# A 16-element average pool: loads and stores issued by GpSimd instead of SyncE, each as a single packet per DMA engine

## The chip, the cores and the metric

The kernel runs on one core of a Trainium2 chip. The metric is the device time of one execution in microseconds (us), and the time of a kernel is the median over several executions. One further execution is recorded by the hardware profiler, and every duration below comes from that record unless it is said otherwise.

Five engines work beside each other on a core, each through its own queue of instructions in program order: TensorE (PE), VectorE (DVE), ScalarE (ACT), GpSimd (POOL) and SyncE (SP). An instruction that has to wait for a semaphore holds up everything behind it in the queue of its engine. Copies between device memory (HBM) and on-chip memory (SBUF) are issued by an instruction on one of these queues and carried out by the 16 DMA engines of the core.

## The reference

The input `x` is float32 of shape 32 x 256 x 4096, and `output_size` is 256. Every output is the mean of 16 neighbouring inputs:

```python
for i in range(output_size):
    start = int(i * length / output_size)
    end = int((i + 1) * length / output_size)
    result[:, :, i] = np.mean(x[:, :, start:end], axis=-1)
```

So 134.2 MB are read and 8.4 MB are written, and each number that is read takes part in one addition.

## The kernel before

Batch and channel are one axis of 8192 rows. A tile holds 4 rows in each of the 128 partitions, which are 128 x 16384 numbers, 64 KB in each partition and 8.39 MB altogether. There are 16 tiles. Tiles 0 to 14 are one region of `x` (`x_many`), in which each partition owns 60 consecutive rows and tile `t` is the t-th group of 4 of them. Tile 15 is a region of its own (`x_last`). The pool of input buffers has `bufs=2`, so two tiles are on the chip at a time, and the load of tile t+2 has to wait until tile t has been read for the last time.

A tile is worked on in five steps:

- Line 70 loads it, one DMA of 128 rows of 64 KB.
- Line 73, on GpSimd, folds the second half of the tile's windows: it adds the upper 8 of the 16 numbers of each window onto the lower 8.
- Line 78, on VectorE, sums the first half's windows over all 16 numbers. It needs the load alone, and runs beside line 73.
- Line 81, on VectorE, sums the second half's windows over the 8 numbers that line 73 left. It is the last reader of the tile.
- Line 84, on ScalarE, multiplies the 1024 sums of each partition by 1/16 in place.

The sums of tiles 0 to 14 stay in `res_many` (60 KB in each partition) and those of tile 15 in `res_last` (4 KB in each partition). There are three stores, all through the helper at line 58. The first writes `res_many` in one DMA and stands in the code between the load of tile 15 and its arithmetic. The other two write partitions 0 to 119 and 120 to 127 of `res_last` at the end. Together they move 8.39 MB, as much as one tile. Each store raises the semaphore `stored`, for which SyncE waits at line 95 before the kernel ends.

The Tile layer decides the order of the instructions on each engine from the code, the buffers and its own estimates, and sets the waits. In the kernel before, SyncE holds only DMAs. The load of tile t+2 waits there for line 81 of tile t and for the landing of the load of tile t. VectorE's order is line 78 and line 81 of tile 0, then of tile 1, and so on. GpSimd holds only the 16 additions of line 73.

Of the kernel before, what the change touches and what calls it, by code (L numbers as in the profile page):

```python
# [1 line left out]

# [4 lines left out]


@with_exitstack
def kernel(  # L10
    ctx: ExitStack,
    tc: tile.TileContext,
    x: bass.AP,
    output_size: int,
    out: bass.AP,
):

    nc = tc.nc
    F32 = mybir.dt.float32
    X = mybir.AxisListType.X

    batch, channels, length = x.shape
    ob, oc, olen = out.shape
    assert ob == batch and oc == channels and olen == output_size
    assert length % output_size == 0
    window = length // output_size  # L30
    hw = window // 2
    inv_w = 1.0 / float(window)

    P = nc.NUM_PARTITIONS
    R = 4
    rows = batch * channels
    assert rows % (P * R) == 0
    ntiles = rows // (P * R)
    many = (ntiles - 1) * R
    cells = R * output_size  # L40
    m = cells // 2
    cols = R * length

    xr = x.rearrange("b c l -> (b c) l")
    orow = out.rearrange("b c o -> (b c) o")
    x_many = xr[0 : P * many, :].rearrange("(p r) l -> p (r l)", p=P, r=many)
    o_many = orow[0 : P * many, :].rearrange("(p r) o -> p (r o)", p=P, r=many)
    x_last = xr[P * many :, :].rearrange("(p r) l -> p (r l)", p=P, r=R)
    o_last = orow[P * many :, :].rearrange("(p r) o -> p (r o)", p=P, r=R)

    res_many = nc.alloc_sbuf_tensor("res_many", [P, (ntiles - 1) * cells], F32, align_bytes=256)
    res_last = nc.alloc_sbuf_tensor("res_last", [P, cells], F32, align_bytes=256)
    inpool = ctx.enter_context(tc.tile_pool(name="inpool", bufs=2))

    stored = nc.alloc_semaphore("stored")

    def store(out, in_):
        ins = nc.sync.dma_start(out=out, in_=in_)
        tc.no_tile_sem_insts.add(ins.ins.name)
        ins.then_inc(stored, 16)  # L60

    for t in range(ntiles):
        last = t == ntiles - 1
        xin = inpool.tile([P, cells, window], F32, name="xin")
        if last:
            res, base, src = res_last, 0, x_last
        else:
            res, base = res_many, t * cells
            src = x_many[:, t * cols : (t + 1) * cols]
        nc.sync.dma_start(out=xin.rearrange("p o w -> p (o w)"), in_=src)  # L70
        if last:
            store(o_many, res_many[:, :])
        nc.gpsimd.tensor_add(  # L73
            out=xin[:, m:cells, 0:hw],
            in0=xin[:, m:cells, 0:hw],
            in1=xin[:, m:cells, hw:window],
        )
        nc.vector.reduce_sum(  # L78
            out=res[:, base : base + m], in_=xin[:, 0:m, :], axis=X
        )  # L80
        nc.vector.reduce_sum(  # L81
            out=res[:, base + m : base + cells], in_=xin[:, m:cells, 0:hw], axis=X
        )
        nc.scalar.mul(  # L84
            out=res[:, base : base + cells],
            in_=res[:, base : base + cells],
            mul=inv_w,
        )
    for lo, hi in ((0, 120), (120, P)):
        store(o_last[lo:hi, :], res_last[lo:hi, :])  # L90

    ctx.pop_all().close()
    tc.close()
    tc.compile()  # L94
    nc.sync.wait_ge(stored, 48)
    nc.sync.sem_clear(stored)


# [1 line left out]
_INS = ['x', 'output_size']  # L100
_OUTS = [((32, 256, 256), 'float32')]

_NUMBERS = {'output_size': 256}


# [26 lines left out]
```

## Time and profile before

| | |
|---|---|
| median of 3 executions | 333.5 us (333.32 to 333.67) |
| the profiled execution | 333.37 us, of which the span of its record is 332.1 us |
| VectorE busy | 209.7 us (63% of the span) |
| GpSimd busy | 139.7 us (42%) |
| ScalarE busy | 18.2 us (5%) |
| DMA packets' time, share of 16 engines' span | 99.4% |
| moved | 142.61 MB, 429 GB/s over the span |

The span is the time from the first to the last recorded event on the core, and 1.27 us of the profiled execution's own time lie outside it. The median of the three executions is 0.13 us above the profiled one. Busy time is the time in which an engine computes; instructions that only issue a DMA, wait or branch are not counted in it. In the profile "SPq" and "POOLq" are the queues of SyncE and GpSimd, that is, their issuing and waiting instructions. `xin<-in_x_dram` is a load of line 70, `out_dram<-res_many` and `out_dram<-res_last` are stores of line 58.

### The profile page before, as it was taken

Reading aid. Unit: us, or ns where it says so; the run is one execution under the profiler, and the core shown is the slowest. Engines: PE = TensorE matmul, PEld = TensorE weight load, DVE = VectorE, ACT = ScalarE, POOL = GpSimd, SP = SyncE. Lnnn points to the kernel's source line nnn. Section 1 sums busy time; section 2 is a strip of 40 time slices with the busy share of each in tenths; the row PEclk is TensorE's granted clock in tenths of the full one; section 3 lists DMA queues with packets and bytes.
Section 4 is the critical chain, followed back from the end, with each engine's and each line's share of the span. In section 5 each row is a group of like instructions: output and inputs, shape, how many; then the busy total and the mean of one; then the engine's idle time right before and its main releaser. Section 6 shows DMA issues by size and latency. Waiting matters only on the chain.

```text
span 332.1 us, 160 instructions
## 1 busy us (share of the span) xinstructions
DVE 209.7 (63%) x32; ACT 18.2 (5%) x17; POOL 139.7 (42%) x20
## 2 busy tenths in 40 slices
DVE  0029396692939669293966939295693929569392
ACT  1000101001010100101010010101000010100001
POOL 0027091542709164270916427090643709063270
DMA  9898999989899998989899998989999898989997
GB/s 379 379 505 379 474 411 426 458 379 505 379 489 395 450 434 379 505 379 505 379 474 411 395 489 379 505 379 489 395 450 434 379 505 379 505 379 474 395 466 307
DMA packets 2599, 142.61 MB, mean 429 GB/s; under 512 B 295, under 2 KB 295, under 8 KB 423
## 3 DMA queue, kind: packets, MB, share of 16 engines
q1 hardware_dynamic: 2599, 142.61, 99.4%
HBM read 134.22 MB, written 8.39 MB: 429 GB/s over the span
## 4 chain that ended last, share of the span: by engine, by line
DMA 66%; POOL 18%; DVE 11%; POOLq 3%; issue 0%; ACT 0%; SPq 0%
DMA xin<-in_x_dram 66%; POOL xin L73 18%; DVE res_many L81 9%; POOLq L94 3%; DVE res_last L81 1%; ACT res_last L84 0%; SPq L70 0%; POOLq L73 0%
## 5 line engine op out<-in xcount | busy, mean ns | idle before, releaser
L73 POOL TENSOR_TENSOR xin<-xin 128x4096 f32<-128x4096 f32 x16 | 139.5, 8719 | 181.7 <-DMA xin<-in_x_dram 181.7
L78 DVE TENSOR_REDUCE res_many<-xin 128x512 f32<-128x8192 f32 x15 | 130.3, 8686 | 107.4 <-DMA xin<-in_x_dram 107.4
L81 DVE TENSOR_REDUCE res_many<-xin 128x512 f32<-128x4096 f32 x15 | 66.3, 4420 | 2.5 <-POOL xin L73 2.3
L84 ACT ACTIVATE res_many<-res_many 128x1024 f32<-128x1024 f32 x15 | 15.9, 1057 | 289.8 <-DVE res_many L81 289.8
L78 DVE TENSOR_REDUCE res_last<-xin 128x512 f32<-128x8192 f32 x1 | 8.7, 8686 | 6.3 <-DMA xin<-in_x_dram 6.3
L81 DVE TENSOR_REDUCE res_last<-xin 128x512 f32<-128x4096 f32 x1 | 4.4, 4420 | 0.2 <-POOL xin L73 0.2
L84 ACT ACTIVATE res_last<-res_last 128x1024 f32<-128x1024 f32 x1 | 1.1, 1057 | 18.5 <-DVE res_last L81 18.5
L84 ACT ACT_TABLE_LOAD x1 | 1.3, 1283 | 0.7 <-PEq L113 0.7
L113 POOL MEMSET const-float32-0.0<- 128x1 f32 x1 | 0.1, 99 | 0.2 <-issue 0.2
L113 POOL MEMSET const-bfloat16-1.0<- 128x1 bf16 x1 | 0.1, 103 | 0.0
L113 POOL MEMSET const-uint8-127<- 128x1 uint8 x1 | 0.1, 103 | 0.0
L113 POOL MEMSET const-float32-1.0<- 128x1 f32 x1 | 0.1, 99 | 0.0
## 6 DMA issues: line engine op xcount, KB each, us to landing
out_dram<-res_many SPq DMA_DIRECT2D x1, 7680.0 KB
out_dram<-res_last SPq DMA_DIRECT2D x1, 480.0 KB
xin<-in_x_dram SPq DMA_DIRECT2D x16, 25.3
out_dram<-res_last SPq DMA_DIRECT2D x1, 32.0 KB
```

Source lines behind the costliest of these rows:

```text
L73: nc.gpsimd.tensor_add(out=xin[:, m:cells, 0:hw], in0=xin[:, m:cells, 0:hw], in1=xin[:, m:cells, hw:window],)
L78: nc.vector.reduce_sum(out=res[:, base : base + m], in_=xin[:, 0:m, :], axis=X)
L81: nc.vector.reduce_sum(out=res[:, base + m : base + cells], in_=xin[:, m:cells, 0:hw], axis=X)
L84: nc.scalar.mul(out=res[:, base : base + cells], in_=res[:, base : base + cells], mul=inv_w,)
L94: tc.compile()
L113: nc = _bacc.Bacc("TRN2", target_bir_lowering=False, num_devices=1)
```

## The change

The loads and the stores are issued from GpSimd's queue instead of SyncE's, and each carries the mark `single_packet=True`, by which the descriptors that one DMA engine gets for a DMA form one packet. Nothing else in the code is edited. SyncE still waits for `stored` at the end.

```diff
     def store(out, in_):
-        ins = nc.sync.dma_start(out=out, in_=in_)
+        ins = nc.gpsimd.dma_start(out=out, in_=in_, single_packet=True)
...
-        nc.sync.dma_start(out=xin.rearrange("p o w -> p (o w)"), in_=src)
+        nc.gpsimd.dma_start(out=xin.rearrange("p o w -> p (o w)"), in_=src, single_packet=True)
         if last:
             store(o_many, res_many[:, :])
```

The Tile layer orders the changed program anew. The orders that it gives GpSimd and VectorE, shortened to the line and the tile (the number is the tile's), are:

```
GpSimd after:   load0 load1 | L73(0) L73(1) load2 load3 | L73(2) L73(3) load4 load5 | ... | L73(14) L73(15) store res_many, store res_last, store res_last
VectorE before: L78(0) L81(0) L78(1) L81(1) | L78(2) L81(2) L78(3) L81(3) | ...
VectorE after:  L78(0) L78(1) L81(0) L81(1) | L78(2) L78(3) L81(2) L81(3) | ... | L78(14) L78(15) L81(14) L81(15)
```

In the changed program load 2 waits for VectorE's third instruction, L81(0), and load 3 for the fourth, L81(1), and so on for each pair. The store of `res_many` waits for line 84 of tile 14, the first store of `res_last` for that of tile 15. ScalarE's order is the same as before.

## The prediction

> **What bounds the kernel now.** I read the page's queue table first, because it says how full the DMA engines are, then the groups of instructions, then the chain that ended last, then SyncE's waits. The first two, from the page:
>
> ```profile
> q1 hardware_dynamic: 2599, 142.61, 99.4%
> ...
> L73 POOL TENSOR_TENSOR xin<-xin 128x4096 f32<-128x4096 f32 x16 | 139.5, 8719 | 181.7 <-DMA xin<-in_x_dram 181.7
> L78 DVE TENSOR_REDUCE res_many<-xin 128x512 f32<-128x8192 f32 x15 | 130.3, 8686 | 107.4 <-DMA xin<-in_x_dram 107.4
> L81 DVE TENSOR_REDUCE res_many<-xin 128x512 f32<-128x4096 f32 x15 | 66.3, 4420 | 2.5 <-POOL xin L73 2.3
> L84 ACT ACTIVATE res_many<-res_many 128x1024 f32<-128x1024 f32 x15 | 15.9, 1057 | 289.8 <-DVE res_many L81 289.8
> ```
>
> The packets fill 99.4% of the time of 16 engines. The idle time of GpSimd and of VectorE ends with the landing of a load. The kernel is bound by its transfers, and the arithmetic hides under them. The chain shows what one round is made of:
>
> ```profile
> 0.74 0.41 SPq L70
> 1.15 0.06 issue
> 1.21 40.77 DMA xin<-in_x_dram
> 41.98 0.07 issue
> 42.05 8.73 POOL xin L73
> 50.78 0.02 issue
> 50.80 4.43 DVE res_many L81
> 55.23 0.02 issue
> 55.25 25.47 DMA xin<-in_x_dram
> ```
>
> Two loads are issued back to back at 0.74, and the second lands at 41.98. So **A = 41.24 us** from the issue of a pair to the landing of its second load when the DMA engines start idle. Then 13.2 us pass until that tile is free and the next load is issued. In the kernel before these 13.2 us cost nothing: the load of the other buffer is already under way, so the new one takes 25.5 us and not the 19.3 that it needs. The timeline gives the pace: VectorE starts on one tile at 254.68, on the next at 273.96 and on the next at 293.27, 19.3 us apart. A pair moves in 38.6 us, and A holds 41.24 - 38.6 = 2.6 us besides, of issue and latency. SyncE's waits:
>
> ```profile
> SPq L70 <- DVE res_many L81: 185.8, 14, 13.3
> SPq L70 <- DMA xin<-in_x_dram: 94.9, 14, 21.1
> SPq L96 <- DMA out_dram<-res_last: 3.0, 1, 3.0
> ```
>
> SyncE's 14 later loads stand waiting for line 81 of the tile two before, up to 13.3 us each. SyncE has nothing else to do, so the wait holds up nobody. In the changed program it does.
>
> **Part 1: the queue that the loads move to.** What is removed: 19 issues on SyncE, 0.33 to 0.41 us each. No engine computes on SyncE, so this frees nothing. What is added: the same 19 issues on GpSimd, whose queue also holds the 16 additions of line 73. The built order puts load 2 and load 3 behind L73(0) and L73(1). L73(1) waits for the landing of load 1. So no load of the next pair can be issued while a load of this pair is in flight, and the DMA engines run empty once in each pair. The cover that hid the 13.2 us is gone: this is the main term.
>
> VectorE's new order counts too. After the second load lands, L78 of the odd tile runs (8.69) beside its L73 (8.72), then L81 of the even tile (4.42), and only then is the even buffer free and the next load issued: 8.69 + 4.42 and some 0.1 of hand-overs, **B = 13.2 us**. L81 of the odd tile follows 4.4 us later and frees the odd buffer. Its load queues behind the first one's 19.3 us of transfer, so those 4.4 us cost nothing; they would cost if the transfer of one tile took less than that.
>
> One pair therefore takes A + B = 41.24 + 13.2 = 54.4 us in place of 38.6.
>
> **Part 2: the stores.** Before, the store of 7.86 MB is issued at 307.67, ahead of the landing of the last load (312.84); it follows that load on the engines and covers the last tile's arithmetic. In the changed order it stands behind L73(15), and waits for line 84 of tile 14, which waits for L81(14), which on VectorE now stands behind L78(15). All the stores (8.39 MB together, one tile's bytes, 19.3 us) come after the last landing with no transfer beside them. The stores of `res_last` wait for line 84 of tile 15, 4.4 us later, under the large store, and cost only their bytes.
>
> **The sum, with issues priced as SyncE's.** The start is at 0.74. Seven periods are 7 x 54.4 = 380.8. The eighth pair lands A later: 0.74 + 380.8 + 41.24 = 422.8. Then B (13.2) and line 84 with its hand-over (1.1) lead to the big store at 437.1. It and the small ones take 19.3 plus the 2.6 of issue and latency, to 459.0. SyncE's wait for `stored` ended at about 331.0 in a span of 332.1, so 1.1 follows: a span of **460.1**.
>
> **Part 3: the price of an issue on GpSimd.** The trace has no DMA issued from GpSimd. Exposed are nine of the 19: the first of each of the 8 pairs and the large store. The others queue under a transfer. Lower bound: the issue vanishes altogether, 0.35 less each, -3 us. Upper bound: it adds the 3.0 us that the whole of a small store's way from issue to landing takes in SyncE's waits, +27 us. I take +0.7, three times SyncE's row in all, since that row is the nearest (same descriptors, 128 rows) and GpSimd is the slower one where it can be compared (8.72 us for 4096 additions per partition, VectorE 4.42 for summing 4096 numbers). That is 9 x 0.7 = 6.3 us, a span of 466.4, and with the 1.3 outside the span **468 us**, 40% over the median. The profiled execution is 0.1 us from that median, so I leave it.
>
> By the Trainium skill's "DMA: Bandwidth & Descriptors" (SWDGE vs HWDGE, and Specifications) descriptors for GpSimd's DMAs are written by a program on its own cores, with about 1 us to the first byte in place of about 0.6. By that page the estimate of this term would be 9 x 0.4 = 3.6 us, a time of 465; no row here shows it.
>
> **Part 4: single packet.** Nothing in the trace shows packets joined. It can save at most what lies between packets, 0.6% of the engines' time by the queue table, 2 us. It can cost an overlap between one packet and the next: at worst the 2.6 us of latency once more for each pair, 8 x 2.6 = 21 us. I take nothing, since at 99.4% the rate is the engines' own either way.
>
> The same page's section Issuing engines are not separate DMA queues says that loads from any engine run on the same 16 DMA engines, and that the choice of issuer saves only the time to issue. Taken alone, that rule would put the changed kernel at 333 to 337 us. The row against it is L73's wait of 181.7 us for loads: the rule speaks of the transfers, and not of what stands ahead of an issue in its queue.
>
> **The rivals.**
>
> *The queue does not bind* (the change does not do what its order says, or loads leave GpSimd's queue ahead of the waiting additions). The loads then go out as before, and joined packets close the gaps of 0.6%: 333.4 - 2.0 = 331.4 us at best, faster. It decides if the issue of load 2 starts before L73(1) has begun. Against it: POOL's additions stand in order behind semaphore waits, and load 2 waits for L81(0), which VectorE now does after L78(1). A faster transfer cannot replace it: 54.4 would have to fall to 38.6, and 16.8 MB to move in 22.8 us, 1.7 times the present pace. 2%.
>
> *The transfers slow down* by a factor of two when GpSimd writes the descriptors. Eight pairs and the stores take 8 x 38.6 + 19.3 = 328 us more: 796 us. For it: nothing in this trace, which has only SyncE's queue. Against it: the DMA engines are the same and the rows are 64 KB. 4%. The page's section Bandwidth has a measured row for loads issued from GpSimd, 79.0 us for 16 MB, where its fit gives 2.0 us plus bytes at 436 GB/s, some 40; the pair here took 41.24 from SyncE, so an estimate by that row would be near this rival, and one by the fit near the forecast.
>
> *GpSimd's issue is as dear as one of its tensor operations*, 8.7 us: 9 x 8.4 = 76 us over 460.1, a time of 537. For it: GpSimd has no shorter row of size here. Against it: a load has 128 rows, L73 4096 numbers in each of 128 partitions. 4%.
>
> **How the numbers follow.** The forecast case has 90%. Its low end is 460.1 + 1.3 - 3 - 2, about 456; its high end is 460.1 + 1.3 + 27, about 488, and 2 more for the overlap that joined packets may lose: 456 to 490. About 5 of the 90% lie outside it, and the other cases hold 10%, so no more than 2 in 10 is left out. A measurement of this kernel can tell about 0.2% from no change. Slower is the forecast and the two dear rivals, 98%; the first rival's 2% is split evenly between faster and the same.
>
> **What would show it.** Right: in the 40 slices the DMA row dips once for each pair, eight times, and its share of the span falls from 99.4% to about 71%; GB/s over the span fall to about 306; the groups of lines 73, 78, 81 and 84 keep their means; line 78 starts in pairs 19 us apart, and a pair every 55 us; GpSimd's queue waits about 13 us for line 81 before each even load; the store of `res_many` starts 14 us after the last landing. A GpSimd issue far from 1 us proves Part 3 wrong. A pair's second landing far from 42 us after its first issue proves Part 4 wrong. If load 2 is issued before L73(1) ends, the main term is wrong.

## The result, and the profile after

The changed kernel takes 465.98 us (median of 4, 465.77 to 466.07) beside 333.51 us before: a ratio of 1.397, with a 95% interval from 1.395 to 1.400. It is slower by 132 us; 468 was predicted, in a range of 456 to 490. The profiled execution took 466.04 us with a span of 464.3, so 1.7 us lie outside the span.

The page of the changed kernel, its queue table and its groups of instructions (busy us, mean ns of one, then the idle time ahead of them and what ended it):

```profile
q0 software_dynamic: 2624, 142.61, 72.2%
...
L78 DVE TENSOR_REDUCE res_many<-xin 128x512 f32<-128x8192 f32 x15 | 130.3, 8686 | 224.8 <-DMA xin<-in_x_dram 224.8
L73 POOL TENSOR_TENSOR xin<-xin 128x4096 f32<-128x4096 f32 x16 | 139.4, 8715 | 227.2 <-DMA xin<-in_x_dram 227.2
L81 DVE TENSOR_REDUCE res_many<-xin 128x512 f32<-128x4096 f32 x15 | 65.6, 4408 | 0.0
...
L70 POOL DMA_DIRECT2D xin<-in_x_dram x16 | 8.9, 558 | 59.0 <-DVE res_many L81 58.2
```

The bytes are the same and the arithmetic is as long as before to within 0.02 us for each instruction. The share of the engines' time that the packets fill fell from 99.4% to 72.2%. The issues, which were SyncE's, are now a row of GpSimd, 0.56 us each.

The changed kernel's timeline, from the landing of one pair's second load to the next pair's:

```profile
42.84 8.69 DVE L78 TENSOR_REDUCE res_many<-xin 128x512 f32<-128x8192 f32 x1 [10.58 <-DMA xin<-in_x_dram]
42.88 8.72 POOL L73 TENSOR_TENSOR xin<-xin 128x4096 f32<-128x4096 f32 x1 [10.55 <-DMA xin<-in_x_dram]
51.44 8.73 DVE L81 TENSOR_REDUCE res_many<-xin 128x512 f32<-128x4096 f32 x2
55.88 1.06 ACT L84 ACTIVATE res_many<-res_many 128x1024 f32<-128x1024 f32 x1 [53.86 <-DVE res_many L81]
56.15 0.57 POOL L70 DMA_DIRECT2D xin<-in_x_dram  x1 [4.55 <-DVE res_many L81]
60.21 1.06 ACT L84 ACTIVATE res_many<-res_many 128x1024 f32<-128x1024 f32 x1 [3.27 <-DVE res_many L81]
60.48 0.53 POOL L70 DMA_DIRECT2D xin<-in_x_dram  x1 [3.75 <-DVE res_many L81]
78.24 8.69 DVE L78 TENSOR_REDUCE res_many<-xin 128x512 f32<-128x8192 f32 x1 [18.06 <-DMA xin<-in_x_dram]
...
97.54 8.69 DVE L78 TENSOR_REDUCE res_many<-xin 128x512 f32<-128x8192 f32 x1 [10.62 <-DMA xin<-in_x_dram]
```

Load 1 has landed when VectorE starts on it at 42.84. Both engines work on tile 1, VectorE sums the second half of tile 0, and only at 56.15 does the first load of the next pair go out, 13.31 us later (B). VectorE starts on the pair's second tile at 97.54, 41.39 us after that (A). A period is 97.54 - 42.84 = 54.70 us. The busy time by stages shows the hole directly (us, then each engine's busy time, granted TensorE clock, DMA share, GB/s):

```profile
42.80:56.20 13.40, 13.36 (x3) 0.32 (x1) 8.77 (x2) 1.00 0.00 0
56.20:59.00 2.80, 2.80 (x1) 0.74 (x1) 0.52 (x1) 1.00 1.09 374
59.00:97.50 38.50, 9.86 (x2) 1.06 (x1) 9.24 (x2) 1.00 0.94 409
```

For 13.4 us the DMA engines move nothing. The changed kernel's last stretch:

```profile
426.25 8.69 DVE L78 TENSOR_REDUCE res_last<-xin 128x512 f32<-128x8192 f32 x1 [10.62 <-DMA xin<-in_x_dram]
...
440.65 0.58 POOL L58 DMA_DIRECT2D out_dram<-res_many  x1 [5.63 <-ACT res_many L84]
443.62 1.06 ACT L84 ACTIVATE res_last<-res_last 128x1024 f32<-128x1024 f32 x1 [3.27 <-DVE res_last L81]
444.98 1.04 POOL L58 DMA_DIRECT2D out_dram<-res_last  x2 [3.75 <-ACT res_last L84]
```

The large store goes out 14.4 us after VectorE starts on the last tile (426.25), with no load beside it, and the span ends 23.7 us later.

### The profile page after: what moved, and what is told of

Read it like the earlier page. It is cut to its first block, busy times and chain, and to the rows that moved or that the text cites. A ratio compares the mean times of both kernels' runs of the same rounds, so it can differ in the third digit from the quotient of the medians.

```text
span 464.3 us, 132 instructions
## 1 busy us (share of the span) xinstructions
DVE 208.2 (45%) x32; ACT 18.2 (4%) x17; POOL 150.2 (32%) x39
## 3 DMA queue, kind: packets, MB, share of 16 engines
q0 software_dynamic: 2624, 142.61, 72.2%
## 4 chain that ended last, share of the span: by engine, by line
DMA 65%; DVE 29%; DVEq 1%; issue 1%; POOL 0%; ACT 0%; POOLq 0%; PEldq 0%
DMA xin<-in_x_dram 65%; DVE res_many L81 14%; DVE res_many L78 13%; DVE res_last L78 2%; DVEq L94 1%; ACT res_last L84 0%; POOL xin L70 0%; POOL out_dram L58 0%; POOLq L94 0%; PEldq L94 0%
## 5 line engine op out<-in xcount | busy, mean ns | idle before, releaser
L73 POOL TENSOR_TENSOR xin<-xin 128x4096 f32<-128x4096 f32 x16 | 139.4, 8715 | 227.2 <-DMA xin<-in_x_dram 227.2
L81 DVE TENSOR_REDUCE res_many<-xin 128x512 f32<-128x4096 f32 x15 | 65.6, 4408 | 0.0
L70 POOL DMA_DIRECT2D xin<-in_x_dram x16 | 8.9, 558 | 59.0 <-DVE res_many L81 58.2
L81 DVE TENSOR_REDUCE res_last<-xin 128x512 f32<-128x4096 f32 x1 | 4.4, 4408 | 0.0
L58 POOL DMA_DIRECT2D out_dram<-res_last x2 | 1.0, 524 | 3.8 <-ACT res_last L84 3.8
## 6 DMA issues: line engine op xcount, KB each, us to landing
out_dram<-res_many POOLq DMA_DIRECT2D x1, 7680.0 KB, 20.1
```

Of the source, the lines that this page charges most:

```text
L58: ins = nc.gpsimd.dma_start(out=out, in_=in_, single_packet=True)
L70: nc.gpsimd.dma_start(out=xin.rearrange("p o w -> p (o w)"), in_=src, single_packet=True)
L73: nc.gpsimd.tensor_add(out=xin[:, m:cells, 0:hw], in0=xin[:, m:cells, 0:hw], in1=xin[:, m:cells, hw:window],)
L81: nc.vector.reduce_sum(out=res[:, base + m : base + cells], in_=xin[:, m:cells, 0:hw], axis=X)
```

## The experiments

My theory: what costs is the order. A load goes out only after the pair's second landing and the arithmetic behind it, so the engines run dry once in each pair; who issues, and the mark, are minor. Its rivals: GpSimd's issue or its descriptors cost by themselves; the packed rows cost; or any DMA suffers in a queue that it shares with arithmetic.

Two orders changed with the edit, GpSimd's and VectorE's. The first three runs write the loop out by hand with the steps as functions (`load`, `fold` for line 73, `first` for 78, `second` for 81, `scale` for 84) and fix the order on every engine. In their profiles L71 is the load, L75 the addition, L83 and L89 the two sums, L95 the multiplication.

**VectorE's paired order, with SyncE issuing.**

```diff
+    with tc.manual_schedule(engines={E.Pool, E.DVE, E.SP, E.Activation}):
+        load(0)
+        load(1)
+        for t in range(0, ntiles, 2):
+            fold(t)
+            first(t)
+            fold(t + 1)
+            first(t + 1)
+            second(t)
+            second(t + 1)
+            scale(t)
+            scale(t + 1)
+            if t + 2 < ntiles:
+                load(t + 2)
+                load(t + 3)
+        store(o_many, res_many[:, :])
```

> SyncE issues every load and store, unmarked, as in the kernel before; only VectorE's order is that of the changed kernel (L78 of both tiles of a pair, then L81 of both). Theory (what costs is that a freed buffer's load goes out only 13 us after the pair's second landing, whoever issues it): a pair takes 41.24 + 13.2 = 54.4 us, eight of them and an uncovered store, so the time is the changed kernel's less what GpSimd's issues add, eight times 0.3 us and 0.5 us at the start: 463 us. Rival (the additions ahead of the loads in GpSimd's queue are the whole cause, VectorE's order is harmless): 333 to 340 us.

458.6 us, a ratio of 1.375 (1.373 to 1.377). The first pairs and the last tile in its timeline:

```profile
41.94 8.69 DVE L83 TENSOR_REDUCE res_many<-xin 128x512 f32<-128x8192 f32 x1 [10.59 <-DMA xin<-in_x_dram]
...
54.98 4.65 SPq L71 DMA_DIRECT2D xin<-in_x_dram  x2
...
96.07 8.69 DVE L83 TENSOR_REDUCE res_many<-xin 128x512 f32<-128x8192 f32 x1 [10.63 <-DMA xin<-in_x_dram]
...
421.01 8.69 DVE L83 TENSOR_REDUCE res_last<-xin 128x512 f32<-128x8192 f32 x1 [10.61 <-DMA xin<-in_x_dram]
```

125 of the 132 us are there without a single DMA on GpSimd, so the rival falls. The period is 54.13 us: B = 54.98 - 41.94 = 13.04, and A = 96.07 - 54.98 = 41.09. GpSimd's period is 0.57 us longer, half of it in B and half in A. The 463 us of my theory were 4.4 too high, because I had taken half that difference for GpSimd's issues and none at the end.

**GpSimd's paired order, with VectorE's put back.** The edit to the loop above, with `nc.gpsimd` and the mark:

```diff
             fold(t)
             first(t)
+            second(t)
+            scale(t)
             fold(t + 1)
             first(t + 1)
-            second(t)
             second(t + 1)
-            scale(t)
             scale(t + 1)
```

> GpSimd issues, marked, in the changed kernel's paired order; only VectorE's order is put back (L78 and L81 of a tile, then the next tile). Theory: load 2 stands behind the addition of tile 1, and is issued when that addition (8.7 us) ends, not 13.3 us after the landing; a pair takes 41.4 + 8.9 = 50.3 us, and the store goes out 5.5 us sooner after the last landing: 466 - 7 x 4.4 - 5.5 = 430 us. Rival 1 (GpSimd issues a DMA while an addition ahead of it still runs): a pair takes about 42 us, 366 us in all. Rival 2 (VectorE's order is the whole cause): 334 us.

428.4 us, a ratio of 1.284 (1.282 to 1.286). Its timeline:

```profile
42.84 8.72 POOL L75 TENSOR_TENSOR xin<-xin 128x4096 f32<-128x4096 f32 x1 [10.58 <-DMA xin<-in_x_dram]
51.50 0.57 POOL L71 DMA_DIRECT2D xin<-in_x_dram  x1
...
93.19 8.72 POOL L75 TENSOR_TENSOR xin<-xin 128x4096 f32<-128x4096 f32 x1 [10.60 <-DMA xin<-in_x_dram]
```

The load's buffer has been free since tile 0 was summed (36.7), and the load has no wait left. It still goes out only as the addition ahead of it ends: its record starts at 51.50, 0.06 us ahead of the addition's recorded end (51.56), and so it is in all seven pairs (0.05 to 0.07 us). So these loads did not go out beside a running addition, and GpSimd's order alone costs 95 us. Either order is enough for a stall; together they cost about the longer of the two (132 us, beside 125 and 95), not the sum, since the addition (8.7 us) runs inside B (13.3).

**Both orders by tile.** GpSimd still issues everything, marked:

```diff
+        for t in range(ntiles):
+            fold(t)
+            first(t)
+            second(t)
+            scale(t)
+            if t + 2 < ntiles:
+                load(t + 2)
+            if t == ntiles - 2:
+                store(o_many, res_many[:, :])
```

> GpSimd issues, marked, as in the changed kernel; both orders are put back: on GpSimd the load of tile t+2 stands right behind the addition of tile t, on VectorE L78 and L81 of a tile come together. Theory (order is all): each load is issued while the other buffer's transfer has 5 us to go, so GpSimd's longer issue is hidden; 0.5 us at the start and some 0.3 us at the end remain: 334.3 us. Rival (the transfers themselves suffer when GpSimd writes the descriptors or when they are one packet): 0.6 us or more for each of 16 tiles, 343 us and over.

336.49 us, a ratio of 1.009 (1.007 to 1.010). 129 of the 132 us are gone with the issuer and the mark left as they are. In its timeline the load of tile 2 goes out between the two additions, 5.8 us ahead of the next landing:

```profile
37.28 0.57 POOL L71 DMA_DIRECT2D xin<-in_x_dram  x1 [4.75 <-DVE res_many L89]
43.06 8.69 DVE L83 TENSOR_REDUCE res_many<-xin 128x512 f32<-128x8192 f32 x1 [6.08 <-DMA xin<-in_x_dram]
...
294.27 8.69 DVE L83 TENSOR_REDUCE res_many<-xin 128x512 f32<-128x8192 f32 x1 [6.09 <-DMA xin<-in_x_dram]
```

From 43.06 to 294.27 are 13 tiles, 19.32 us each, the pace of before. The 3.0 us that are left are 2.2 more than expected. In the spans the difference is 2.7 (334.8 and 332.1): the first pair lands 1.1 us later, the last load another 0.1, and from that landing to the span's end it takes 1.5 longer.

**The stores back on SyncE**, as a check on that:

```diff
-        ins = nc.gpsimd.dma_start(out=out, in_=in_, single_packet=True)
+        ins = nc.sync.dma_start(out=out, in_=in_)
```

> Loads on GpSimd, marked, with both orders put back by tile; stores on SyncE, unmarked. Theory (the 3.0 us that were left there are 1.0 us at the first load and 2 us in and behind the stores): the end gets back SyncE's 4.1 us from issue to the end in place of 5.1 and the last load still shares the engines with the store from another queue: 335.5 us. Rival (all that is left comes from the loads on GpSimd): 336.5 us as with the stores there.

335.27 us (ratio 1.005, 1.004 to 1.007): 1.2 us came back with the stores. That is the size expected, but it came another way: the expectation had the last load share the engines with a store from another queue in both runs, and it does so only here. VectorE starts on the last tile at 316.10, 2.0 us later than in the run before, and from there to the end of the span it takes 18.0 us in place of 20.7. What delays the landing is shown with the stores below.

**The mark.** The changed kernel without it (the store's line likewise), and the kernel before with it alone:

```diff
-        nc.gpsimd.dma_start(out=xin.rearrange("p o w -> p (o w)"), in_=src, single_packet=True)
+        nc.gpsimd.dma_start(out=xin.rearrange("p o w -> p (o w)"), in_=src)
```

> The changed kernel without the single-packet mark. Theory (the mark does nothing here): 466.0 us within 0.5 us. Rival (the mark joins what had to be apart, or saves gaps between packets): 2 us or more away from it, either side, up to 21 us less.

> The kernel before with the single-packet mark alone; SyncE issues. Theory (the mark does nothing where 64 KB rows already fill 99.4% of the engines' time): 333.5 us within 0.3 us. Rival (it closes the gaps of 0.6%): 331.5 to 333 us.

On GpSimd 466.46 us without the mark beside 465.98 with it: the four times without it lie 0.1% above the four with it, but the intervals of the ratios, 1.396 to 1.401 and 1.395 to 1.400, lie over each other. On SyncE 333.52 us with the mark, ratio 1.0002 (0.9993 to 1.0011). The record lists 2624 packets on GpSimd's queue with the mark and without it, and 2599 on SyncE's both times. So on neither queue does the mark change the time by more than some 0.1%, and no view here shows descriptors that were joined by it.

**Another queue that holds arithmetic.** ScalarE issues (the store's line likewise), and nothing else is edited:

```diff
-        nc.sync.dma_start(out=xin.rearrange("p o w -> p (o w)"), in_=src)
+        nc.scalar.dma_start(out=xin.rearrange("p o w -> p (o w)"), in_=src)
```

> ScalarE issues all loads and stores, unmarked. Its queue also holds the 16 multiplications of line 84, but the load of tile t+2 stands right behind the multiplication of tile t, and VectorE's order stays by tile. Theory (sharing a queue with compute costs nothing where the order leaves the load close behind its own release): issue at 14.4 us after a landing in place of 13.2, still 5 us ahead of the next landing: 333.5 to 334 us. Rival (any queue with waiting compute delays the loads): 16 x 1.1 = 18 us more, 351 us.

333.71 us, ratio 1.0008 (0.9998 to 1.0017): no difference. The Tile layer left its orders by tile, and each load stands right behind the multiplication of the tile that it replaces:

```profile
35.92 1.06 ACT L84 ACTIVATE res_many<-res_many 128x1024 f32<-128x1024 f32 x1 [32.98 <-DVE res_many L81]
35.98 0.33 ACTq L70 DMA_DIRECT2D xin<-in_x_dram  x1
```

On ScalarE, sharing a queue with arithmetic costs nothing here. It is not GpSimd's case, though: the load goes out 0.06 us after the multiplication ahead of it has started and 1.0 us before that ends, so at 13.3 us after the landing and not at the 14.4 that were expected. On GpSimd the loads went out only as the addition ahead of them ended. That a queue with additions need not cost much is shown by the run with both orders by tile.

**The stores alone on GpSimd**, marked and unmarked:

```diff
-        ins = nc.sync.dma_start(out=out, in_=in_)
+        ins = nc.gpsimd.dma_start(out=out, in_=in_, single_packet=True)
```

> Only the stores are issued by GpSimd, marked; loads stay on SyncE. The large store stands there between the additions of tiles 14 and 15. Theory: it goes out 14.7 us after the landing of tile 14, 4.6 us ahead of the last landing, so only the dearer issue of the last stores is seen: 333.5 to 335 us. Rival (a store on GpSimd holds up the last addition behind it): the last tile's sums come up to 5 us later, 337 to 339 us.

> Only the stores on GpSimd, without the mark. With it the last load landed 2.2 us later than before, since the large store on its own queue was carried out beside it. Theory (two queues share the engines packet by packet, and a packet is one row either way): 336.3 us again, within 0.5. Rival (joined rows let the store push ahead of the load's last rows): the last load lands where it did before, 334 to 335 us.

336.27 us (ratio 1.0085, 1.0071 to 1.0099) and 336.17 us. Both parts of the first expectation missed the cause. The last tiles in the kernel before, and with the marked stores on GpSimd:

```profile
312.86 8.69 DVE L78 TENSOR_REDUCE res_last<-xin 128x512 f32<-128x8192 f32 x1 [6.31 <-DMA xin<-in_x_dram]
```

```profile
307.98 0.74 POOL L58 DMA_DIRECT2D out_dram<-res_many  x1 [5.85 <-ACT res_many L84]
315.05 8.69 DVE L78 TENSOR_REDUCE res_last<-xin 128x512 f32<-128x8192 f32 x1 [8.47 <-DMA xin<-in_x_dram]
```

The last addition is not held up by the store ahead of it: the store's issue is over at 308.7, and the addition starts when its load has landed. It is the load that lands at 315.02 where it was 312.84 before. The packets in the traces show that its data are not late: its last 64 KB row is through at 312.42, and at 312.47 before. But a load is closed by 16 writes of 4 bytes, and in these runs it counts as landed 0.3 to 0.4 us after the last of the 16. Before, with the store on the same queue, all 16 go ahead of the store's rows, the last at 312.47. With the store on a queue of its own, three of the 16 are sent only at 314.24 to 314.68, when the first rows of the store (2.27 us each) are through. In the unmarked run it is 11 of the 16, and the landing is at 315.19; with the loads on GpSimd and the stores on SyncE it is all 16, and 316.08. So the store does not move beside the load's data; it slips in ahead of the writes that close the load, and the mark has no part in it.

**GpSimd's queue with nothing but DMAs.** VectorE sums whole tiles, and the additions are gone; from GpSimd with the mark, and then from SyncE without it:

```diff
-        nc.gpsimd.tensor_add(
...
         nc.vector.reduce_sum(
-            out=res[:, base : base + m], in_=xin[:, 0:m, :], axis=X
+            out=res[:, base : base + cells], in_=xin[:, :, :], axis=X
         )
-        nc.vector.reduce_sum(
-            out=res[:, base + m : base + cells], in_=xin[:, m:cells, 0:hw], axis=X
-        )
```

> The changed kernel without the additions on GpSimd: VectorE sums whole windows of the whole tile in one instruction (17.4 us by the two halves' 8.69), so GpSimd's queue holds nothing but the DMAs. Theory (the queue's other work is what costs): load t+2 is issued 17.7 us after landing t, some 1.5 us ahead of landing t+1, so a tile still takes 19.3 to 19.8 us; the last tile's arithmetic takes 4.2 us more than before: 337 to 345 us. Rival (a DMA issued from GpSimd is dear in itself, in issue or in transfer): over 350 us.

> As the run with nothing but DMAs on GpSimd's queue (359.65 us where 337 to 345 were expected), but SyncE issues, unmarked. That run's loads went out 1.8 us ahead of the landing of the other buffer's load, and the one behind a short lead landed 22 to 23 us after the one before it in place of 19.3. Theory (a lead shorter than the 2.5 us from issue to full flow lets the engines run empty, whoever issues): SyncE's lead is about half a us longer, 2.3 us, so part of the loss stays: 342 to 355 us. Rival (GpSimd's issue itself hurts the transfers): all of it goes, 337 to 338 us.

From GpSimd three executions took 359.01, 359.34 and 359.95 us (1.078, 1.076 to 1.080) and a fourth, the profiled one, 365.34. That is over the 337 to 345 of my theory and where the rival stood, "over 350". But SyncE takes 352.82 us (1.058, 1.054 to 1.063; 351.25 to 354.17) with the same long sum, where the rival of that run had 337 to 338. So most of the loss, 19.2 us, comes with the long sum, whoever issues. GpSimd adds 6.5 (359.34 - 352.82), or some 0.47 for each of the 14 loads that wait; where in a round it goes is not shown. SyncE's timeline, and its line of the queue table:

```profile
22.60 17.22 DVE L73 TENSOR_REDUCE res_many<-xin 128x1024 f32<-128x16384 f32 x1 [22.60 <-DMA xin<-in_x_dram]
...
41.89 17.22 DVE L73 TENSOR_REDUCE res_many<-xin 128x1024 f32<-128x16384 f32 x1 [2.07 <-DMA xin<-in_x_dram]
...
63.32 17.22 DVE L73 TENSOR_REDUCE res_many<-xin 128x1024 f32<-128x16384 f32 x1 [4.22 <-DMA xin<-in_x_dram]
...
83.24 17.22 DVE L73 TENSOR_REDUCE res_many<-xin 128x1024 f32<-128x16384 f32 x1 [2.70 <-DMA xin<-in_x_dram]
```

```profile
q1 hardware_dynamic: 2599, 142.61, 96.7%
```

The buffer is free at 39.82, 2.0 us ahead of the landing at 41.87, and the load that then goes out lands 21.4 us after that landing in place of 19.3. The next one has a lead of 4.2 us and lands 19.9 after. My first expectation had counted a lead of 1.5 us as enough. A holds 2.5 us besides its 38.6 of transfer (41.09 in SyncE's paired run), and engines that run dry behind a shorter lead were my theory for the second run. Its time lies in the range given, but the mechanism is shown only in part. The packets' time is 96.7% of 350.7 = 339.1 us where it was 99.4% of 332.1 = 330.1, so of the 18.6 us that the span is longer, 9.6 are time in which the engines moved nothing, and 9.0 are the same packets taking longer. Nor does the lead decide by itself: over the 14 tiles it lies between 2.0 and 5.6 us, and about 2.0 stood ahead of 21.4, 22.9 and 19.8 us, 2.8 ahead of 19.3 and 4.6 ahead of 20.1. What makes the packets longer, and what decides at the same lead, stays open.

## Why the prediction was right

- **Part 1, the main term.** A + B was right in mechanism and size: 54.4 us predicted with issues at SyncE's price, 54.13 measured in the run that has this order on SyncE. B was set 0.16 too high and A 0.15: its 41.24 came from the first pair of the kernel before, and the second pair of this run has 41.09. I wrote that the cause was the load's place behind the additions, and that VectorE's order "counts too". The runs put them the other way round: VectorE's order alone makes 125 us, GpSimd's alone 95, and VectorE's is the one that sets B. The sum came out because B was reckoned from VectorE's order (8.69 + 4.42) all the same.
- **Part 2, the stores.** The large store was predicted 14.3 us after the last landing and went out at 14.4.
- **The sum at SyncE's price.** 460.1 us of span were predicted, and the SyncE run has 456.8: 1.8 us by the last landing (421.0 where 422.8 was worked out) and 1.5 behind it.
- **Part 3, GpSimd's issue.** 6.3 us were taken; the spans of the two paired runs differ by 464.3 - 456.8 = 7.5. By place: 0.9 at the first pair, 4.3 over the seven periods (54.77 and 54.15 us on average, 0.62 each) and 2.3 from the last landing on. An issue takes 0.56 us in place of SyncE's 0.33, and 0.29 us pass between the end of what it waits for and its start (SyncE's 0.02); the sign for this part was an issue of about 1 us, and the two together are 0.85. I had 0.7 for each of nine exposed issues. That is close for the pairs (0.62), but the end, which holds one exposed issue, cost 2.3. That the total came out 2 us from the measured one is in part luck: the sum ahead of it was 3.3 us too high, the issues 1.2 too low, and the time outside the span was 1.7 and not 1.3. One reading was off without weight: SyncE's issues go down to 0.29 us, not 0.33.
- The estimate by the Trainium skill's "DMA: Bandwidth & Descriptors" (SWDGE vs HWDGE, and Specifications), 0.4 us for each issue, lies below the 0.62 that the two paired runs differ by for each pair; 0.7 lay above it. Its section Issuing engines are not separate DMA queues speaks of the transfers and of the time to issue from several engines at once. For the transfers the run with both orders by tile agrees, at 19.32 us a tile from GpSimd's queue as from SyncE's; the section says nothing of the queue's order, which is where nearly all of the 132 us are. The 79.0 us that its section Bandwidth gives for 16 MB issued from GpSimd do not hold here: 16.8 MB took 41.39. By the rate of 425 GB/s that stands in the same row it would be an estimate of 39.5, and by the page's own fit (Anatomy of one DMA) of 2.0 us plus bytes at 436 GB/s 40.5; both are near the measured time.
- **Part 4, the mark.** Nothing was taken, and no more than some 0.1% was measured on either queue. The part had put the worst case at 21 us, but the range's upper end holds only 2 for it; the two do not fit together, and the measurement did not come near either.
- **The signs.** The share of 72.2% and 307 GB/s answer to "about 71%" and "about 306". One sign was put wrongly: I wrote that GpSimd's queue waits 13 us for line 81 before an even load. The timeline shows 4.55, because the first 8.7 are its own addition. Load 2 goes out at 56.15, behind the end of L73(1) at 51.60, as the sign for the main term had it.
- **The rivals.** That the queue does not bind is refuted by the run with VectorE's order put back, where a load without a wait stood 8.7 us behind a running addition. Half pace and an issue as dear as an addition are refuted by A and by the 558 ns of the changed kernel's row.

## What to carry to other kernels

Before moving a DMA to another queue, write down what stands ahead of it there and what its own wait hangs on, then follow the chain from the last landing to the next issue: with two buffers, each microsecond by which the issue comes after that landing, and the fixed time from issue to flow, is lost once a round. Look at the order of all engines in the built program, since the scheduler may reorder one that the edit does not touch; here VectorE's new order was enough for most of the loss. If GpSimd must issue the loads, put each right behind the release of its buffer, which gave nearly 6 us of lead here (5.8 ahead of the next landing): that took the loss from 132 us to 3. Shorter leads, 2.0 to 5.6 us in SyncE's run with the long sum, hid some loads and not others.

## What was not expected of the hardware

A lead of 2.0 to 5.6 us did not reliably hide a load even on SyncE: with it, tiles took 20.5 us on average in place of 19.3 (14 tiles from 41.89 to 328.67), and about half of the added time was packets that took longer. A store on a queue of its own put the landing of the load issued before it back by 2.2 us without delaying its data, by going ahead of the writes that close the load; a store on the same queue had put it back by 0.3 (19.59 against 19.31 us between the last landings). And a load behind a running instruction went out 0.06 us after that instruction's start on ScalarE, but only at its end on GpSimd.
